# Dilated attention beside Strassen projections on one core: visits four steps later, the factors' transposition last in a visit, its read-back issued by POOL

## The chip, the cores and the metric

One Trainium2 chip; the kernel runs on one of its cores. The engines of a core that matter here are PE (TensorE, matrix products), DVE (VectorE) and ACT (ScalarE, both elementwise), POOL (GpSimd, which here mostly issues DMAs) and SP (SyncE, which only issues DMAs). The metric is the time of one execution in microseconds (us), the median of several runs.

## The reference

One layer of a bidirectional encoder over 1024 positions with 1024 features, in float32. Attention in three groups of four heads (window and dilation 128/1, 512/4, 2048/16) and a gated linear attention are mixed, followed by a squared-ReLU MLP. Cut to the part that matters here:

```
for gi, (win, dil) in enumerate(ATTN_PAIRS):
    o_g, lse_g = _dilated_group(aq[:, :, hs], ak[:, :, hs], av[:, :, hs], bias, dil, k_side)
    outs.append(o_g)
    lses.append(lse_g)
mix_w = jax.nn.softmax(jnp.stack(lses, axis=0), axis=0)
y_attn = jnp.sum(mix_w[..., None] * jnp.stack(outs, axis=0), axis=0)
...
merged = (jax.nn.sigmoid(gate_a) * (y_attn @ w_attn_branch[l])
          + jax.nn.sigmoid(gate_g) * (y_gla @ w_gla_branch[l]))
x = _layernorm(ALPHA * x + merged @ w_out[l], ln1_g[l], ln1_b[l])
```

The three groups' outputs for a head are added with weights that follow from their softmax denominators. These weights are the "factors" of this document.

## The kernel before

**The large products.** All large products are made of float32 split into two parts (a high part of fewer bits, and the rest), so each logical product of a 128x128 block with 512 columns is three matmuls (lines 102 to 104). The projections of the input are done in pairs of 128-row blocks by Strassen's scheme: seven products of four blocks each, so a *step* is 12 matmuls on PE, and a pair has seven steps. The list `steps` holds 10 steps that are left of two first pairs, and then seven for each of 14 pairs, 108 in all. A step has sides to be prepared three steps ahead (sums on DVE, then the split: cast on ACT, difference on DVE, line 152), and its product leaves PSUM by DVE (line 646) or ACT (lines 651, 671) into a tile `cr` or `cu`; finished blocks go to DRAM (`spill`, line 625, SP). The raw weights `praw` and `pwhi` come by SP (line 612).

**The attention tiles.** The pairs that project queries and keys come first, group 2, then 1, then 0, and the pairs of the gates last. Beside the pairs from there on run 24 attention tiles, `att(g, t)`: group 2's eight tiles of 128 queries, then group 1's, then group 0's. A tile has eight parts. `load` fetches queries `aq` and keys `ak` from `spill` (line 776, POOL). `scores` fetches the values `av` (lines 787 to 801, POOL), multiplies queries with keys into PSUM `sc` (line 809), adds the bias and finds the maximum on DVE (line 815, into `e` and `sm`), and takes the exponential on ACT (line 820). `turned` transposes `e` on PE (line 832, into `tr`) and copies it to `et`. `values` multiplies it with the values on PE (line 847) into the PSUM tile `avp`, columns 0 and 1 of three. For groups 1 and 2 the result is stored as it is (line 861). For group 0 it is weighted: `W` holds the factors of all three groups for this tile, spread over the partitions; DVE multiplies its first part with the result in PSUM (line 863), the second and third part with the stored results of the other groups, read back into `R` (line 871), adds them (line 872, `mixed`), and POOL stores the sum (line 873, `yadr`).

**The factors.** For a tile of group 0, `weigh` and `shares` work out the factors from the denominators in a chain of small DVE operations (lines 884 to 900, tile `f`). `spread` transposes them on PE (line 905) into column 2 of the same PSUM tile `avp`, ACT copies them to `fT` (line 906) and stores them in DRAM (line 907, `fdr`, issued by ACT); `loadw` reads them back into `W`, each row spread over 64 partitions (line 913). `W` has one buffer.

**The order.** A *visit* `visit(i)` does one part each of neighbouring tiles: `load` of tile i+1, `spread` of i-1, `values` of i-2, `scores` of i and `turned` of i-1. There are 26 visits; visit i stands ahead of the step whose number is given by a formula, from step 25 to step 96, every two or three steps. `weigh` comes one step after the visit, `shares` two, `loadw` of tile i-1 one, and from visit 17 on, every second visit, `quarter` (line 929, SP) reads the others' results for two tiles. The matmuls keep the written order by being told after which instruction they may issue (`issued["pe"]` is the last matmul of a large product, `issued["small"]` the last of a visit); other engines take their work in an order that the scheduler of the framework sets at build time, each engine in order. `W` was read back by SP.

**After the pairs.** One step after the last pair but one ends, the attention's memory is given up, and the tiles `ya` (from `yadr`) and `yg` for the merge are read and split beside the last seven steps (line 1002, SP). The merge then multiplies them with the branch weights.

Of the kernel before, what the change touches and what calls it, by code (L numbers as in the profile page):

```python
# [72 lines left out]
def build(tc, io):  # L73
    nc = tc.nc
    V, G, A, T, SP = nc.vector, nc.gpsimd, nc.scalar, nc.tensor, nc.sync
    P = Pools(tc)
    issued = {}
# [109 lines left out]
    for k in range(KT):  # L187
        n = {0: 1, 1: 1, 2: 2, 4: 2, 6: 2}.get(k)
# [532 lines left out]
    a, b = p0["steps"][1], p0["steps"][4]  # L721
# [30 lines left out]
    R, W = ap_.tile([128, 2, 2, 256], F32, name="R"), ap_.tile([128, 3, 2, 128], F32, name="W")  # L752
# [15 lines left out]
    def att(g, t):  # L768

        w, b0, k0 = window(g, t)  # L770
        b = {}
# [129 lines left out]

        def spread():
            if g == 0:
                with tc.issue_after(issued["pe"].ins):
                    issued["small"] = T.transpose(av[0:12, 2], b["f"][:, 0:3].rearrange("p g h -> p (g h)"), ident)
                A.copy(fT, av[0:12, 2])
                A.dma_start(fdr[t].rearrange("i r n -> r i n"), fT)

        def loadw():
            if g == 0:  # L910
                for i in range(2):
                    one = fdr[t, i:i + 1].rearrange("i r n -> i (r n)")
                    SP.dma_start(W[64 * i:64 * i + 64].rearrange("p g b n -> p (g b n)"), one.to_broadcast([64, 768]))

        return load, scores, turned, values, weigh, shares, spread, loadw

    def stats(g):
        for u in range(2):
            G.dma_start(s12[:, 4 * u:4 * u + 4, g - 1],
                        smdr[g - 1, 512 * u:512 * u + 512].rearrange("(t p) w -> p t w", p=128))  # L920

    def quarter(n):
        u, q = n // 2, n % 2
        for g in (1, 2):
            c = ORD[g]
            for pr in range(2):
                src = numdr[g - 1, pr].rearrange("p (c u q j) -> p u q c j", c=c, u=2, q=2)[:, u, q]
                dst = R[:, g - 1, pr].rearrange("p (c j) -> p c j", c=c)
                SP.dma_start(dst, src)
# [31 lines left out]

    def visit(i):

        for n, part in ((i + 1, 0), (i - 1, 6), (i - 2, 3), (i, 1), (i - 1, 2)):
            if 0 <= n < 24:
                tiles[n][part]()
        if i in (12, 16):
            stats(2 if i == 12 else 1)


    n0 = len(steps) + 14
    for p in projs[2:]:
        steps += p["steps"]
    n1 = len(steps) - 7
    units = {}
    for i in range(26):
        n = n0 + 1 + i * (n1 - n0) // 27
        units.setdefault(n, []).append(lambda i=i: visit(i))
        for k, part, later in ((i, 4, 1), (i, 5, 2), (i - 1, 7, 1)):
            if 0 <= k < 24 and (later == 1 or k > 15):  # L980
                units.setdefault(n + later, []).append(lambda k=k, part=part: tiles[k][part]())
        if i in (17, 19, 21, 23):
            units[n + 1].append(lambda i=i: quarter((i - 17) // 2))
    for i in range(8):

        n = n0 - 18 + i * 3 // 2
# [839 lines left out]
def make(arrays):  # L1826
    import concourse.bacc as _bacc
    nc = _bacc.Bacc("TRN2", target_bir_lowering=False, num_devices=1, dynamic_dma_scratch_size=1024)
    io = {}
    for n, a in arrays.items():  # L1830
        io[n] = nc.dram_tensor(f"in_{n}", a.shape, mybir.dt.from_np(a.dtype), kind="ExternalInput").ap()
    io["out"] = nc.dram_tensor("out_0", (S, D), F32, kind="ExternalOutput").ap()
    with tile.TileContext(nc, schedule_with_timeline_sim=True) as tc:
        build(tc, io)
    return nc
# [8 lines left out]
```

## Time and profile before

| | us |
|---|---|
| median of 3 runs (1393.45 to 1394.84) | 1394.82 |
| the profiled execution | 1393.93 |
| its span, first to last instruction | 1392.1 |
| PE busy | 1360.8 |
| DVE busy | 1008.3 |
| ACT busy | 629.5 |
| POOL busy | 105.1 |

The visits run from 299 us (the first scores) to 578 us (the last values) of the span. The page of the profile has the busy time of each engine, and the chain of work that ended last. The view of waits adds up, for each engine, who it waited for, and the timeline gives single instructions with their start, their duration and the idle time ahead of them with its releaser in square brackets. A row with "x8" stands for eight instructions in a row. An instruction that waits for several results is put down to the one that came last. The durations of matmuls overlap, since they are pipelined: the distance from one start to the next is what one costs. The mean granted clock of PE over the span is 0.993 of full speed.

### The profile page before, as it was taken

The numbers are of one execution on the slowest core, as the hardware profiler recorded it, in microseconds if no ns is written. First come the engines' busy times: TensorE is split into PE (matmuls) and PEld (weight loads), VectorE is DVE, ScalarE is ACT, GpSimd is POOL, SyncE is SP. The second block draws the span as 40 slices with busy tenths as digits, with TensorE's granted clock in tenths as the row PEclk, the third lists the DMA queues.
The fourth block names the chain that finished last, engine by engine and source line by source line (L and its number), as shares of the span: only waits on it lengthen the run. The fifth ranks groups of instructions, "written<-read, shape, count | busy, mean of one in ns | idle before, by whom it ended". The sixth has DMA issues, their size and how long they took to land.

```text
span 1392.1 us, 19096 instructions
## 1 busy us (share of the span) xinstructions
PE 1360.8 (98%) x6829; PEld 1133.4 (81%) x6829; DVE 1008.3 (72%) x1748; ACT 629.5 (45%) x1207; POOL 105.1 (8%) x157
## 2 busy tenths in 40 slices
PE   9999999979999998999999999999999999999998
PEld 7989998857877776788888888888888888888886
DVE  6377768756566576577666787788867897786988
ACT  5346645324444343354426655555556533333333
POOL 0000100022333221000001000000000000000002
PEclk9999999989999999999999999999999999999999
DMA  7262326755455564565763655666555965545313
GB/s 255 61 204 71 120 79 218 201 168 154 149 157 170 152 179 134 155 214 184 265 236 112 237 192 186 228 217 213 199 216 160 359 224 166 163 122 165 102 35 121
DMA packets 119747, 241.77 MB, mean 174 GB/s; under 512 B 33269, under 2 KB 42133, under 8 KB 119652
## 3 DMA queue, kind: packets, MB, share of 16 engines
q1 hardware_dynamic: 113044, 223.71, 48.8%
q0 software_dynamic: 6176, 16.39, 4.0%
q8 instruction: 54, 0.88, 0.3%
q10 hardware_dynamic: 432, 0.44, 0.1%
q14 instruction: 41, 0.34, 0.1%
HBM read 163.81 MB, written 77.73 MB: 174 GB/s over the span
## 4 chain that ended last, share of the span: by engine, by line
PE 93%; DVE 3%; ACT 2%; DMA 1%; issue 1%; SPq 0%; ACTq 0%; DVEq 0%; POOLq 0%
PE ps L102 18%; PE ps L103 18%; PE ps L104 18%; PE mm L102 10%; PE mm L103 10%; PE mm L104 10%; PE sc L809 2%; PE avp L847 2%; PE tr L832 2%; ACT xr L1235 1%; PE sc L409 0%; PE tr L379 0%; DVE cr L646 0%; DMA pwhi<-in_wfm 0%; DMA spill<-cr 0%
## 5 line engine op out<-in xcount | busy, mean ns | idle before, releaser
L1216 ACT CAST T<-hp 128x1024 fp32r<-128x1024 f32 x36 | 37.9, 1052 | 109.9 <-PE ps L103 70.4
L103 PE MATMUL mm<-wlo,x 128*128 128x272 f32 (+1 forms) x240 | 74.5, 311 | 0.7 <-DVE wlo L95 0.7
L102 PE MATMUL mm<-whi,x 128*128 128x272 f32 (+1 forms) x240 | 75.0, 313 | 0.0
L104 PE MATMUL mm<-whi,x 128*128 128x272 f32 (+1 forms) x240 | 74.7, 311 | 0.0
L820 ACT ACTIVATE e<-e,sm 128x256 f32<-128x256 f32 (+2 forms) x96 | 43.3, 453 | 68.2 <-DVE sm L815 59.5
L103 PE MATMUL ps<-B,B 128*128 128x512 f32 x160 | 62.2, 389 | 0.0
L104 PE MATMUL ps<-B,B 128*128 128x512 f32 x160 | 62.2, 389 | 0.0
L102 PE MATMUL ps<-B,B 128*128 128x512 f32 x160 | 60.9, 390 | 0.5 <-ACT B L1216 0.5
L103 PE MATMUL ps<-T,T 128*128 128x512 f32 x144 | 56.0, 389 | 0.0
L104 PE MATMUL ps<-T,T 128*128 128x512 f32 x144 | 56.0, 389 | 0.0
L102 PE MATMUL ps<-B,T 128*128 128x512 f32 x144 | 56.0, 389 | 0.0
L104 PE MATMUL ps<-B,T 128*128 128x512 f32 x144 | 56.0, 389 | 0.0
L103 PE MATMUL ps<-B,T 128*128 128x512 f32 x144 | 56.0, 389 | 0.0
L102 PE MATMUL ps<-T,T 128*128 128x512 f32 x144 | 56.0, 389 | 0.0
L1217 DVE TENSOR_TENSOR T<-hp,T 128x1024 fp32r<-128x1024 f32 x36 | 43.9, 1219 | 15.1 <-ACT T L1216 15.0
L1617 DVE TENSOR_TENSOR acc<-ps,acc 128x512 f32<-128x512 f32 x68 | 45.5, 683 | 12.8 <-PE ps L104 12.2
L646 DVE TENSOR_TENSOR cr<-cu,mm 128x512 f32<-128x512 f32 x44 | 35.2, 800 | 25.5 <-PE mm L104 25.3
L1722 POOL TENSOR_TENSOR mv<-mv,mhalf 128x1 f32<-128x1 f32 x8 | 7.0, 881 | 607.3 <-DVE mv L1721 605.8
L102 PE MATMUL mm<-x,pwlo 128*128 128x512 f32 x128 | 50.7, 396 | 1.4 <-ACT cu L651 1.4
L102 PE MATMUL ps<-T,fraw 128*128 128x512 f32 x128 | 49.6, 390 | 0.4 <-ACT T L1216 0.4
L103 PE MATMUL mm<-x,pwlo 128*128 128x512 f32 x128 | 49.9, 390 | 0.0
L104 PE MATMUL mm<-x,pwlo 128*128 128x512 f32 x128 | 49.9, 390 | 0.0
(498 smaller groups left out, 4191.1 us busy)
## 6 DMA issues: line engine op xcount, KB each, us to landing
hdr<-c SPq DMA_DIRECT2D x112, 256.0 KB, 2.2
hp<-hdr SPq DMA_DIRECT2D x56, 512.0 KB, 3.5
spill<-cr SPq DMA_DIRECT2D x64, 256.0 KB, 3.3
praw<-in_wfm SPq DMA_DIRECT2D x16, 512.0 KB, 5.4
pwhi<-in_wfm SPq DMA_DIRECT2D x16, 512.0 KB, 5.0
gate<-spill SPq DMA_DIRECT2D x32, 256.0 KB, 3.7
wa<-in_w SPq DMA_DIRECT2D x16, 512.0 KB, 5.3
wb<-in_w SPq DMA_DIRECT2D x16, 512.0 KB, 7.2
```

What stands on the lines that cost most here:

```text
L102: T.matmul(ps, lh, rh, start=first and i == 0, stop=False, skip_group_check=more)
L103: T.matmul(ps, lh, rl, start=False, stop=False, skip_group_check=more)
L104: issued["pe"] = T.matmul(ps, ll, rh, start=False, stop=last and i == n - 1, skip_group_check=more)
L646: issued["add"] = V.tensor_tensor(o, a, b, op=OP.add)
L809: mm = T.matmul(sps[i][:, pr, 0:w], q[ps_, pr], k[ps_, pr, 0:w], start=True, stop=True)
L820: issued["exp"] = A.activation(e, e, AF.Exp, bias=sm[:, h:h + 1], scale=-1.0, accum_out=sm[:, 4 + h:5 + h])
L832: T.transpose(tp[0:hi - lo, pr, j], b["e"][i][:, pr, lo:hi], ident)
L847: return T.matmul(av[64 * i:64 * i + 64, pr], vv[:, h * 64:h * 64 + 64], b["et"][i][p0:p0 + vv.shape[0], pr, j], start=j == pr == 0, stop= ...
L1216: A.copy(o[:, 0], src)
L1217: V.tensor_tensor(o[:, 1], src, o[:, 0].bitcast(F32), op=OP.subtract)
L1235: A.activation(q[i][:, k], tp[:, k], AF.Identity, bias=cols[:, c + 8:c + 9], scale=cols[:, c:c + 1])
L1617: V.tensor_tensor(m, p, m, op=OP.add)
```

## The change

Three edits. The formula of the visits' steps now begins at n0 + 5 in place of n0 + 1 and ends four steps later, at step 100; the two lines below are all of it. In a visit, `spread` of tile i-1 moves from second to last place, and its matmul is ordered after the visit's last small one instead of after the last large one. The read-back of the factors is issued by POOL instead of SP.

```
-                with tc.issue_after(issued["pe"].ins):
+                with tc.issue_after(issued["small"].ins):
                     issued["small"] = T.transpose(av[0:12, 2], b["f"][:, 0:3].rearrange("p g h -> p (g h)"), ident)
...
-                    SP.dma_start(W[64 * i:64 * i + 64].rearrange("p g b n -> p (g b n)"), one.to_broadcast([64, 768]))
+                    G.dma_start(W[64 * i:64 * i + 64].rearrange("p g b n -> p (g b n)"), one.to_broadcast([64, 768]))
...
-        for n, part in ((i + 1, 0), (i - 1, 6), (i - 2, 3), (i, 1), (i - 1, 2)):
+        for n, part in ((i + 1, 0), (i - 2, 3), (i, 1), (i - 1, 2), (i - 1, 6)):
...
-        n = n0 + 1 + i * (n1 - n0) // 27
+        n = n0 + 5 + i * (n1 - 6 - n0) // 25
```

What moves is seen in the built programs, whose rows stand in the order in which an engine takes them (line, operation, output and inputs, shape).

On PE, where the first scores stand (`x` and `xT` are the split input, `pw` and `px` the sides of a pair). Before:

```order
L104 MATMUL mm<-xT_2101,pwlo 128x512
...
L102 MATMUL mm<-x_94,px 128x512
...
L104 MATMUL mm<-x_94,px 128x512
L809 MATMUL sc<-ak_2251,aq_2248 128x128 x4
L102 MATMUL mm<-xT_2207,pwhi 128x512
```

And with the change:

```order
L104 MATMUL mm<-x_94,px 128x512
L102 MATMUL mm<-xT_2207,pwhi 128x512
...
L102 MATMUL mm<-xT_2086,pwhi 128x512
...
L104 MATMUL mm<-xT_1981,pwlo 128x512
L809 MATMUL sc<-ak_2251,aq_2248 128x128 x4
L102 MATMUL mm<-xT_2101,pwlo 128x512
```

The scores of the first tile stand behind 48 large matmuls more: the 1302 of the pairs that were ahead of them are 1350 now. All visits move by about as much; the last values stand behind 2202 in place of 2154.

On PE, in a visit of group 0 (the fourth with a transposition of factors). Before:

```order
L104 MATMUL mm<-xT_2224,pwhi 128x512
L905 MATMUL avp<-ident,f_2267 12x128
L847 MATMUL avp<-et_2260,av_2253 64x128
L847 MATMUL avp<-et_2261,av_2253 64x128
...
L809 MATMUL sc<-ak_2251,aq_2250 128x256 x4
L832 MATMUL tr<-ident,e_2258 128x128 x4
L832 MATMUL tr<-ident,e_2259 128x128 x4
L102 MATMUL mm<-x_93,pwlo 128x512
```

With the change:

```order
L104 MATMUL mm<-xT_1981,pwlo 128x512
L847 MATMUL avp<-et_2260,av_2253 64x128
L847 MATMUL avp<-et_2261,av_2253 64x128
...
L809 MATMUL sc<-ak_2251,aq_2250 128x256 x4
L832 MATMUL tr<-ident,e_2258 128x128 x4
L832 MATMUL tr<-ident,e_2259 128x128 x4
L905 MATMUL avp<-ident,f_2267 12x128
L102 MATMUL mm<-xT_2101,pwlo 128x512
```

The transposition now stands behind the visit's 8 matmuls of values, 4 of scores and 8 transpositions, and the large matmuls stand behind it. Between two transpositions stand 36 large matmuls, and once 24, before and now.

On ACT, in the same visit, around the copy of the factors and their store. Before:

```order
L651 COPY cu_2105<-mm 128x512
L906 COPY fT<-avp 12x128
L907 DMA fdr<-fT 6x2x128
L820 ACTIVATE e_2256,sm_2265<-e_2256,sm_2265 128x256 x2
L839 COPY et_2260<-tr 128x512
L820 ACTIVATE e_2257,sm_2265<-e_2257,sm_2265 128x256 x2
L888 ACTIVATE f_2266<-f_2266 128x12
```

With the change:

```order
L839 COPY et_2260<-tr 128x512
L820 ACTIVATE e_2256,sm_2265<-e_2256,sm_2265 128x256
L906 COPY fT<-avp 12x128
L820 ACTIVATE e_2256,sm_2265<-e_2256,sm_2265 128x256
L820 ACTIVATE e_2257,sm_2265<-e_2257,sm_2265 128x256 x2
L907 DMA fdr<-fT 6x2x128
L151 CAST pwlo<-pwhi 128x512
```

The copy and the store stood ahead of the four exponentials of the visit's scores; the store now stands behind all four. In the other visits it stands behind two to four of them, and in the last behind none, as there are no scores. On DVE L863 still stands ahead of the L815 of the same visit that those exponentials need.

## The prediction

> **What bounds the kernel now.** I read the page first, then the sum of waits of PE, then PE's timeline around each long wait.
>
> ```profile
> span 1392.1 us, 19096 instructions
> PE 1360.8 (98%) x6829; PEld 1133.4 (81%) x6829; DVE 1008.3 (72%) x1748; ACT 629.5 (45%) x1207; POOL 105.1 (8%) x157
> PE 93%; DVE 3%; ACT 2%; DMA 1%; issue 1%; SPq 0%; ACTq 0%; DVEq 0%; POOLq 0%
> ```
>
> PE is the bound from end to end: it is busy 98% of the span and carries 93% of the chain that ended last. A change that adds or removes no matmul can only move the 31 us in which PE is idle, and the time in which its clock is low. The next view lists the waits of PE, longest sum first (total, times, longest):
>
> ```profile
> PE sc L809 <- DMA ak<-spill: 9.6, 1, 9.6
> PE avp L905 <- DVE f L900: 7.2, 5, 2.2
> PE avp L847 <- ACT fT L906: 4.1, 8, 1.0
> PE mm L102 <- ACT cu L651: 1.4, 1, 1.4
> ```
>
> All four lie between 290 and 580 us. The first is the wait of the first scores for their keys; the next two are the transposition of the factors at the head of a visit, and the values that follow it. Each of the three belongs to an edit.
>
> **Edit 1: the visits begin four steps later.** In PE's timeline (start, duration, instruction, idle time before it):
>
> ```profile
> 289.41 0.39 PE L104 MATMUL mm<-x,px 128*128 128x512 f32 x1
> 299.40 1.23 PE L809 MATMUL sc<-ak,aq 64*128 64x128 f32 x8 [9.61 <-DMA ak<-spill]
> 300.56 0.79 PE L102 MATMUL mm<-xT,pwhi 128*128 128x512 f32 x1
> 304.43 0.39 PE L102 MATMUL mm<-xT,pwhi 128*128 128x512 f32 x1
> 307.96 0.71 PE L809 MATMUL sc<-ak,aq 64*128 64x128 f32 x8
> 308.61 0.66 PE L832 MATMUL tr<-ident,e 128*128 128x128 f32 x4
> 463.67 0.48 PE L102 MATMUL mm<-xT,pwlo 128*128 128x512 f32 x1
> 471.74 0.39 PE L104 MATMUL mm<-x,px 128*128 128x512 f32 x1
> 296.59 1.43 POOL L776 DMA_DIRECT2D ak<-spill  x2 [8.52 <-DMA spill<-cr]
> ```
>
> The 36 matmuls from 463.67 to 471.74 run undisturbed, so one costs 8.07 / 35 = 0.23 us and a step of twelve 2.75 us. Four steps are 48 matmuls, 11.0 us; as the rows of the order show, exactly these 48 now stand ahead of the first scores. PE would come to them at 289.8 + 11.0 = 300.8. The keys' load is issued by POOL at 296.59, when the projections have landed in DRAM; neither that projection nor its load is moved, and the scores began at 299.40. So the wait goes, with 1.4 us to spare. After it the clock was low: nine matmuls took 304.43 - 300.56 = 3.87 us where 2.07 is usual, and the scores 1.16 us to the next start where 0.65 is usual: 2.3 us. **Edit 1 is worth 9.6 + 2.3 = 11.9 us.** The matmuls put in between hide the load; should the write or the load be later by more than 1.4 us, the rest is waited for again.
>
> At the far end the last visit moves from 12 steps before the end of the projections to 8, which is 96 matmuls or 22 us of cover for what follows it: three products on DVE, the write of the mixed tile and its reading by the merge. Before, SP had these reads behind twelve steps; I cost this at nothing, as the two DMAs (under 5 us each, by the rows of DMAs below) and some 4 us of DVE need about 14. Without that cover the merge would wait for the difference.
>
> **Edit 2: the transposition last in a visit.** Here are the first, one middle and the last of the eight visits that have it:
>
> ```profile
> 473.75 0.28 PE L905 MATMUL avp<-ident,f 128*12 128x128 f32 x1 [1.62 <-DVE f L900]
> 474.37 1.49 PE L847 MATMUL avp<-et,av 128*64 128x128 f32 x16 [0.34 <-ACT fT L906]
> 475.79 2.08 PE L809 MATMUL sc<-ak,aq 64*128 64x256 f32 x8
> 512.64 0.27 PE L905 MATMUL avp<-ident,f 128*12 128x128 f32 x1
> 513.25 1.09 PE L847 MATMUL avp<-et,av 128*64 128x128 f32 x16 [0.34 <-ACT fT L906]
> 516.19 0.47 PE L102 MATMUL mm<-x,pwlo 128*128 128x512 f32 x1
> 566.22 0.28 PE L905 MATMUL avp<-ident,f 128*12 128x128 f32 x1 [0.86 <-DVE f L900]
> 577.10 1.24 PE L847 MATMUL avp<-et,av 128*64 128x128 f32 x16
> ```
>
> A visit without waits takes 516.19 - 512.64 - 0.34 = 3.2 us, so from one transposition to the next PE needs 8.3 + 3.2 = 11.5 us where 36 matmuls lie between, and 8.8 where 24 do, which happens once. Seven intervals should take 6 x 11.5 + 8.8 = 77.8 us; 473.75 to 566.22 is 92.5. With the 1.6 before the first, these visits lose 16.3 us: idle time, and low clock after some of it (scores of 2.08 us where 1.1 is usual). Last in the visit, the transposition comes 3 us later, past the longest wait for L900 (2.2), and the values find the copy of fT long done. Of the 16.3 only the 1.4 of L651 has no link to the edit, so **14.9 us go**.
>
> But a new wait takes their place. Values and factors share one PSUM tile: that is why L847 waits for the copy of fT above. So the transposition must now wait until DVE has read the values that stand just ahead of it (L863), and L863 needs W of that tile. W is what the transposition of the visit before wrote, copied, stored and read back. This ring has to close within one interval. On ACT the store (L907) moves behind the exponentials of the same visit, which wait for DVE's L815, which stand behind L863. The rows:
>
> ```profile
> 502.61 0.42 DVE L863 TENSOR_TENSOR W<-avp,W 128x256 f32<-128x256 f32 x1
> 504.88 0.51 ACT L820 ACTIVATE e<-e,sm 128x256 f32<-128x256 f32 x1 [3.52 <-DVE sm L815]
> 506.85 0.49 ACT L820 ACTIVATE e<-e,sm 128x256 f32<-128x256 f32 x1
> 474.35 1.30 ACTq L907 DMA_DIRECT2D fdr<-fT  x1
> 478.00 1.12 SPq L913 DMA_DIRECT2D W<-fdr  x2
> 566.82 0.71 ACTq L907 DMA_DIRECT2D fdr<-fT  x1
> 567.40 0.95 SPq L91 DMA_DIRECT2D raw<-in_wb  x2
> SPq L913 <- DMA fdr<-fT: 0.2, 1, 0.2
> 518.04 0.43 DVE L872 TENSOR_TENSOR mixed<-W 128x256 f32<-128x256 f32 x1
> 518.87 0.73 POOL L873 DMA_DIRECT2D yadr<-mixed  x1 [1.56 <-DVE sm L815]
> W<-fdr SPq DMA_DIRECT2D x16, 192.0 KB, 4.2
> av<-vdr POOLq DMA_DIRECT2D x5, 256.0 KB, 3.1
> ak<-spill POOLq DMA_DIRECT2D x4, 256.0 KB, 4.6
> ```
>
> From L863 to the end of the fourth exponential is 507.3 - 502.6 = 4.7 us; in half of the visits L907 stands behind fewer of them or one DVE operation less, so 4.5. The store takes between 1.7 us (568.35 + 0.2 - 566.82, where SP came late to its wait) and 3.65 (474.35 to 478.00); I take the middle, 2.7. POOL picks up a result 518.87 - 518.47 = 0.4 us after it is there. The first of two W loads is issued for 0.73 us, and the second lands after 3.1 to 4.6 us by other loads of POOL, 4.2 by SP's own; no row shows W from POOL, so I take 3.6. **The ring is 4.5 + 2.7 + 0.4 + 0.7 + 3.6 = 11.9 us**, between 10.4 and 13.9. Against the intervals: the first is covered (its L907 hangs on no L863, 0.7 us spare), the short one waits 11.9 - 8.8 - 0.7 = 2.4, five others 0.4 each: 4.4, and 1.7 of low clock after the long one (as the visit at 473.75 lost some 1.6 after 1.62 idle). **The ring costs 6.1 us**; at 10.4 about nothing, at 13.9 some 18 and low clock on top.
>
> DVE too stands still while L863 waits, with everything behind it:
>
> ```profile
> 500.00:520.00 20.00, 18.52 (x119) 14.75 (x120) 16.10 (x55) 7.62 (x25) 5.80 (x8) 1.00 0.70 201
> ```
>
> 16.1 us of work in 20 (the third number after the window's length) leaves some 2 us per interval, about what the ring takes; behind L863 are sums and splits for matmuls of at least one step later, so I add nothing.
>
> **Edit 3: POOL issues the read-back.** SP loses 16 issues and its waits for them; nothing on PE waited for SP, so the gain is nothing. On POOL the loads stand behind the store of the mixed tile of the same visit (4 us after L863 at most, while the store of fT lands at 7.2) and ahead of loads that are needed a visit later. POOL is busy 5.8 of 20 us.
>
> [...]
>
> **Sum.** 11.9 + 14.9 - 6.1 = 20.7 us. The profiled execution took 1393.93 us, 1.8 more than its span; the median of the runs is 1394.82, so 0.9 above it. 1394.8 - 20.7 gives **1374 us**.
>
> **Rivals.**
> 1. The ring hides (10.4 us): only the low figure of the store speaks for it. 11.9 + 14.9, less a rest of 1: 1369.
> 2. The ring is long (13 us): the store lands late beside SP's large loads, as at 474.35, W as late as ak. Waits: 0.4 + 4.2 + 5 x 1.5 = 12.1, low clock 4 or 5: 17 in place of 6, 1385.
> 3. Edit 1 does not do what it says: SP's queue or the loads put in front make the keys late by as much again, and the first scores wait at their new place. Against it: that projection, its store and POOL's load keep their order. Gain 14.9 - 6.1 = 9: 1386.
> 4. Slower: POOL, in order, comes to W only when an earlier DMA has landed. The nearest row:
>
> ```profile
> 509.88 0.73 POOL L873 DMA_DIRECT2D yadr<-mixed  x1 [4.41 <-DVE f L898]
> 505.10 0.42 DVE L872 TENSOR_TENSOR mixed<-W 128x256 f32<-128x256 f32 x1
> ```
>
> There POOL was 4.4 us late for a result of 505.5. Once per visit this makes the ring 16.3: waits of 3.7 + 7.5 + 5 x 4.8 = 35 and some 9 of low clock, 44 against the 26.8 removed: 1412. It decides from a ring of 14 to 15 us on. Of eight such stores one was that late, so it is unlikely for all.
>
> **Chances.** Forecast (1371 to 1381) 0.52, ring hidden 0.20, long ring 0.13, first wait stays 0.08, slower 0.07. 0.2% is 2.8 us, about what a measurement of this kernel can tell from no change. Faster by more than that: the first four but 0.02 of the long ring, 0.91; within it 0.03; slower 0.06. The range goes from 1367, where all the idle time of these visits is gone (28 us), to 1388; above lie the slower case and the worst of the long ring.
>
> **What would show it.** Step 1: no wait of L809 for ak, and full clock from 290 to 310. Step 2: no wait of L905 for L900 nor of L847 for L906, but one of L905 for L863, longest at the visit after 24 matmuls, and DVE idle ahead of L863 until W has landed. The distance from one L863 to the next, some 12 us, is the ring; from 14 on I am wrong in size, from 15 in sign. Step 3: POOL's W loads start 0.4 us after the store of fT has landed. A wait of the first product of the merge for ya would show the far end uncovered.

## The result, and the profile after

| | before | after |
|---|---|---|
| median, us | 1394.13 (4 runs, 1393.43 to 1394.84) | 1376.13 (4 runs, 1374.96 to 1376.83) |
| the profiled execution, us | 1393.93 | 1376.83 |
| its span, us | 1392.1 | 1375.0 |

The ratio is 0.9870, with a 95% interval of 0.9853 to 0.9887: 18 us less, against a forecast of 20.7 and a time of 1374. The head of the page after:

```profile
span 1375.0 us, 19093 instructions
PE 1359.5 (99%) x6829; PEld 1132.6 (82%) x6829; DVE 1008.8 (73%) x1748; ACT 630.0 (46%) x1207; POOL 113.7 (8%) x173
```

PE's busy time is what it was, and the span is nearer to it by 16 us: the time came from PE's idle time and its low clock, as foretold. The waits of PE after, longest sum first (total, times, longest):

```profile
PE avp L905 <- DVE W L863: 4.9, 2, 2.5
PE mm L102 <- DVE cu L646: 1.4, 1, 1.4
```

The wait for the keys (9.6), that for L900 (7.2) and that for L906 (4.1) are gone. What stands there is the wait of L905 for L863, twice. The stages show where the time went. These windows of before give length, busy PE, PEld, DVE, ACT and POOL, then PE's granted clock, the share of the DMA engines and GB/s:

```profile
234.00:290.00 56.00, 55.79 (x246) 45.68 (x244) 44.79 (x69) 19.00 (x34) 4.00 (x6) 1.00 0.72 218
290.00:465.00 175.00, 165.60 (x954) 132.00 (x955) 101.13 (x277) 71.05 (x213) 58.60 (x86) 0.97 0.48 146
465.00:580.00 115.00, 102.36 (x588) 79.93 (x586) 79.04 (x258) 40.48 (x117) 17.81 (x25) 0.97 0.54 158
```

And the same windows after:

```profile
234.00:290.00 56.00, 54.62 (x241) 44.75 (x240) 43.29 (x67) 18.58 (x33) 3.47 (x5) 1.00 0.70 208
290.00:465.00 175.00, 174.72 (x1001) 139.32 (x1000) 107.80 (x279) 73.05 (x213) 57.60 (x85) 1.00 0.51 160
465.00:580.00 115.00, 110.10 (x631) 87.67 (x630) 83.71 (x275) 46.14 (x129) 28.70 (x45) 0.97 0.56 162
```

In the stage from 290 on, where groups 2 and 1 are visited, PE's idle time falls from 9.4 us to 0.3 and the clock rises from 0.97 to 1.00. In the stage with group 0, idle time falls from 12.6 to 4.9 us, but the clock stays at 0.97. The window ahead of both, which lies ahead of the visits, has 1.2 us more of idle time after. PE's timeline after, at the first scores, at the first large matmul behind visit 16 (the last visit ahead of group 0's factors), at six of the eight transpositions of group 0's visits, and at the first large matmul behind visit 25, the last:

```profile
303.18 0.71 PE L809 MATMUL sc<-ak,aq 64*128 64x128 f32 x8
465.59 0.48 PE L102 MATMUL mm<-xT,pwhi 128*128 128x512 f32 x1
488.53 0.27 PE L905 MATMUL avp<-ident,f 128*12 128x128 f32 x1
499.88 0.27 PE L905 MATMUL avp<-ident,f 128*12 128x128 f32 x1 [2.47 <-DVE W L863]
512.90 0.27 PE L905 MATMUL avp<-ident,f 128*12 128x128 f32 x1
526.93 0.28 PE L905 MATMUL avp<-ident,f 128*12 128x128 f32 x1 [2.43 <-DVE W L863]
539.99 0.27 PE L905 MATMUL avp<-ident,f 128*12 128x128 f32 x1
551.21 0.27 PE L905 MATMUL avp<-ident,f 128*12 128x128 f32 x1
571.15 0.50 PE L102 MATMUL mm<-x,px 128*128 128x512 f32 x1
```

The end of the same stretch before:

```profile
578.28 0.50 PE L102 MATMUL mm<-x,pwlo 128*128 128x512 f32 x1
```

From 539.99 to 551.21 nothing waits: 11.22 us is what 36 large matmuls and a visit take. After each of the two waits the next distance is longer than that by 1.8 us (13.02, 13.06): low clock, granted at 0.53 from 500.46 to 504.10 and from 527.74 to 531.39. The first wait stands at the interval with 24 large matmuls. Each "distance" here is from the start of one transposition to the start of the next.

The distance from the first transposition to the last is no fair measure, because the transposition has changed its place in the visit and so other work lies in between. The *stretch of group 0's visits* is: from the first large matmul behind visit 16 to the first behind visit 25 the work of PE is the same in both kernels. It took 114.6 us before (463.67, a row shown in the prediction, to 578.28) and takes 105.6 us after (465.59 to 571.15).

What the parts gave in these two executions: PE was 2.6 us late by 285 already, as the same product started at 284.06 before and at 286.66 after. With that, and the 48 matmuls of the edit (10.9 us), the first scores would have come at 312.9; they came at 303.18, so 9.7 us is gained there, and 1.9 from there to the second scores (8.56 us before, 6.70 after). **The first two visits gave 11.6 us**; edit 1 was foretold at 11.9. **The visits of group 0 gave 9.0 us**; edit 2 was foretold at 8.8. Together 20.6; less the 2.6 lost ahead of them and 0.9 behind them, this is the 17.1 us between the spans. These are the gains of two stages, and not yet those of two edits: the next section shows that edit 1 also shortens the second stage.

### The profile page after: what moved, and what is told of

It is laid out like the page before. It is cut to its first block, busy times and chain, and to the rows that moved or that the text cites. A ratio compares the mean times of both kernels' runs of the same rounds, so it can differ in the third digit from the quotient of the medians.

```text
span 1375.0 us, 19093 instructions
## 1 busy us (share of the span) xinstructions
PE 1359.5 (99%) x6829; PEld 1132.6 (82%) x6829; DVE 1008.8 (73%) x1748; ACT 630.0 (46%) x1207; POOL 113.7 (8%) x173
## 4 chain that ended last, share of the span: by engine, by line
PE 61%; ACT 1%; DMA 1%; issue 1%; DVE 1%; POOL 0%; POOLq 0%; DVEq 0%; ACTq 0%
PE ps L102 18%; PE ps L103 18%; PE ps L104 18%; PE mm L102 2%; PE mm L104 2%; PE mm L103 2%; ACT xr L1235 1%; DMA pwhi<-in_wfm 1%; PE ps L1232 0%; PE avp L847 0%; PE ps L1743 0%; DMA W<-fdr 0%; DMA fdr<-fT 0%; PE tr L832 0%; PE ps L1739 0%
## 5 line engine op out<-in xcount | busy, mean ns | idle before, releaser
L102 PE MATMUL mm<-whi,x 128*128 128x272 f32 (+1 forms) x240 | 75.0, 312 | 0.0
L102 PE MATMUL ps<-B,B 128*128 128x512 f32 x160 | 61.0, 390 | 0.5 <-ACT B L1216 0.5
L646 DVE TENSOR_TENSOR cr<-cu,mm 128x512 f32<-128x512 f32 x44 | 35.3, 802 | 32.4 <-PE mm L104 32.2
L102 PE MATMUL ps<-T,T 128*128 128x512 f32 x144 | 56.1, 389 | 0.0
L102 PE MATMUL ps<-B,T 128*128 128x512 f32 x144 | 56.1, 389 | 0.0
L102 PE MATMUL mm<-x,pwlo 128*128 128x512 f32 x128 | 51.5, 402 | 1.4 <-DVE cu L646 1.4
L102 PE MATMUL ps<-T,fraw 128*128 128x512 f32 x128 | 49.6, 390 | 0.4 <-ACT T L1216 0.4
```

The costliest lines, as they stand in the source:

```text
L102: T.matmul(ps, lh, rh, start=first and i == 0, stop=False, skip_group_check=more)
L646: issued["add"] = V.tensor_tensor(o, a, b, op=OP.add)
```

## The experiments

### Which edit gives what

Each of four kernels has some of the three edits and nothing else.

Edit 1 alone: the kernel before with

```
-        n = n0 + 1 + i * (n1 - n0) // 27
+        n = n0 + 5 + i * (n1 - 6 - n0) // 25
```

> Only the visits begin four steps later; the transposition of the factors stays first, SP reads them back. By the two traces the first scores lose their wait of 9.6 us and 1.9 us of low clock, 11.6 us in all, and the eight visits of group 0 keep what they lost before: 1394.1 - 11.6 = 1382.5 us, within 1.5. Rival: the late start also brings the last visits nearer to the merge or upsets SP's queue, and part is given back: 1385 or more. Rival: edit 1 carries nearly all of the gain: 1377 or less.

Edits 2 and 3: the changed kernel with the line above undone.

> The transposition last in a visit and the read-back by POOL, with the visits at their old steps. The first scores wait for their keys as before (9 to 10 us). In the eight visits of group 0 the traces show 17.4 us of waits and low clock gone and 8.4 come (two waits of L905 for L863, 2.5 us each, and 1.8 of low clock behind each): 1394.1 - 9.0 = 1385.1 us, within 1.5. Rival: the two edits help only with the late start: 1390 or more.

Edits 1 and 2: the changed kernel with

```
-                    G.dma_start(W[64 * i:64 * i + 64]...
+                    SP.dma_start(W[64 * i:64 * i + 64]...
```

> The changed kernel with the read-back issued by SP again. The prediction has edit 3 at nothing: 1376 us, within 1. Rival: SP, in order, waits for the store of fT, which now lands later than before, with raw weights and stores queued behind it, or comes to it late from them; W lands 2 us or more later, the ring closes in 13 to 14 us, L905 waits for L863 in most visits: 1382 to 1386.

Edits 1 and 3: the changed kernel with `spread` second in a visit again, ordered after `issued["pe"]`.

> The changed kernel with the transposition of the factors first in a visit again. The 17.4 us of the group-0 visits come back (waits of L905 for L900, of L847 for L906) and the 8.4 of the ring go: 1376.1 + 9.0 = 1385.1 if POOL's read-back helps nothing; by the run with edit 1 alone the same 1382.5 to 1385. Rival: the waits for L900 came of SP's W loads and POOL's load removes part of them: 1380 or less.

| edits | median, us | runs from to | ratio to before | 95% interval | stretch of group 0's visits, us |
|---|---|---|---|---|---|
| none | 1394.55 | 1393.07 to 1395.29 | 1 | | 114.6 |
| 1 | 1381.41 | 1378.82 to 1382.74 | 0.9906 | 0.9891 to 0.9922 | 109.5 |
| 2, 3 | 1387.04 | 1385.69 to 1390.19 | 0.9950 | 0.9938 to 0.9963 | 106.6 |
| 1, 2 | 1381.31 | 1376.81 to 1383.00 | 0.9899 | 0.9883 to 0.9916 | 108.7 |
| 1, 3 | 1387.87 | 1386.21 to 1388.21 | 0.9951 | 0.9939 to 0.9964 | 118.5 |
| 1, 2, 3 | 1376.13 | 1374.96 to 1376.83 | 0.9870 | 0.9853 to 0.9887 | 105.6 |

The time without edits was taken beside the four partial kernels; all three edits were measured earlier, against 1394.13. The last column is read from the one profiled execution of each kernel, over the stretch defined above.

Edit 1 alone gives 13.1 us, by its interval 10.9 to 15.2. Edits 2 and 3 without it give 7.5 (5.2 to 8.6), a little under what was expected. These would add up to 20.6, and all three give 18.0, because they overlap: edit 1 alone was expected to leave the visits of group 0 as they were, but takes 5.1 us off their stretch. Edits 2 and 3 take 8.1 us off it without edit 1, and 3.9 on top of edit 1. Why the later steps help these visits was not followed up.

On top of edit 1, edit 3 alone costs 6.5 us (9.0 in the stretch), and edits 2 and 3 together give 5.3 (3.9 in the stretch). Edit 2 alone gives nothing by the medians (0.8 in the stretch). This last is the least sure: the five runs with edits 1 and 2 lie 6 us apart, the fastest of them (1376.81, the profiled one) is about as fast as the changed kernel, and the two intervals overlap a little. That edit 3 is worth nothing is wrong: without edit 2 it costs, and with edit 2 it gains by the medians, and by 3.1 us in the stretch.

Why edit 3 alone costs time is seen in PE's rows around one transposition. With edit 1 alone:

```profile
511.52 0.27 PE L905 MATMUL avp<-ident,f 128*12 128x128 f32 x1
523.55 0.27 PE L905 MATMUL avp<-ident,f 128*12 128x128 f32 x1
536.05 0.27 PE L905 MATMUL avp<-ident,f 128*12 128x128 f32 x1
```

With edits 1 and 3:

```profile
511.88 0.27 PE L905 MATMUL avp<-ident,f 128*12 128x128 f32 x1
529.30 0.38 PE L905 MATMUL avp<-ident,f 128*12 128x128 f32 x1 [5.23 <-DVE f L900]
542.96 0.27 PE L905 MATMUL avp<-ident,f 128*12 128x128 f32 x1
```

These two intervals are 6.6 us longer, of the 9.0 by which all eight visits are longer in these two executions. On DVE, in the kernel with edits 1 and 3, the sum of the raw weights L633 stands there ahead of the last two operations of the factors, L899 and L900 (the last is shown):

```profile
527.75 0.69 DVE L633 TENSOR_TENSOR psum<-pwhi 128x512 f32<-128x512 f32 x1 [4.65 <-DMA pwhi<-in_wfm]
529.08 0.17 DVE L900 TENSOR_TENSOR f<-f 128x12 f32<-128x12 f32 x1
```

And with edit 1 alone it stands behind them:

```profile
522.99 0.17 DVE L900 TENSOR_TENSOR f<-f 128x12 f32<-128x12 f32 x1
526.71 0.69 DVE L633 TENSOR_TENSOR psum<-pwhi 128x512 f32<-128x512 f32 x1 [3.56 <-DMA pwhi<-in_wfm]
```

The raw weights are late in both (3.6 and 4.7 us of waiting). In one the factors are done ahead of this wait, in the other they stand behind it. The read-back itself stands in neither chain: its engine made the scheduler write DVE's list in another order, and these few rows are the only difference between DVE's lists in the two programs (L639, an operation on the same raw weights, moves with L633).

### Edit 3: the order on DVE, or POOL's issue

With edits 1 and 2, L863 stood at one place ahead of L898 to L900 of the next tile, and L905 waited 4.9 us for L900. The next kernel is that one, with L863 told to issue behind the last L900:

```
+                issued["fac"] = V.tensor_tensor(f[:, 0:3], f[:, 0:3], f[:, 4:5]...
...
-            o = V.tensor_tensor(W[:, 0], av[:, 0:2], W[:, 0], op=OP.mult)
+            with tc.issue_after(issued.get("fac", issued["add"]).ins): o = V.tensor_tensor(W[:, 0], av[:, 0:2], W[:, 0], op=OP.mult)
```

> The kernel with edits 1 and 2 (SP issues the read-back), and one thing more: L863 is told to issue behind the last L900. Only one place of DVE's list changes by it: there L863, which waits for W, stood ahead of L898 to L900 of the next tile, and L905 waited 4.9 us for L900. Now these stand ahead of it, as with POOL's read-back. Theory: edit 3 gained by the order on DVE alone: 1376 us as with all three edits, at least 3 us below the 1381.3 of the kernel with edits 1 and 2. Rival: POOL's own issue, off SP's queue, is what gains: 1381 stays.

Measured: 1377.12 us (1374.87 to 1380.20), ratio 0.9879, 0.9865 to 0.9892. The median falls by 4.2 of the 5.2 us, but the intervals of the two kernels overlap, and their profiled executions took 1376.62 and 1376.81 us. The trace does not bear the theory out. PE's row at that place, with edits 1 and 2:

```profile
500.43 0.38 PE L905 MATMUL avp<-ident,f 128*12 128x128 f32 x1 [4.92 <-DVE f L900]
```

And with the forced order:

```profile
498.75 0.38 PE L905 MATMUL avp<-ident,f 128*12 128x128 f32 x1 [3.88 <-DVE W L863]
```

The wait for L900 is gone, and one for W, 1.0 us shorter, has its place: SP's two issues of W took 1.84 us there, and L863 waited 4.5 us for W to land (the slowest load of W in that kernel took 5.3 us, the median 3.4). With POOL the wait of L905 was 2.47. So at this place, in these executions, 1.0 us goes with the order and 1.4 with the read-back itself; the rest of the 5 us is within the spread of these runs (6 us with edits 1 and 2). Over the stretch of group 0's visits the forced order takes 108.3 us, against 108.7 without it and 105.6 with POOL: 0.4 of 3.1 us. What edit 3 gains on top of edits 1 and 2 is therefore not shown to be the order on DVE; how it divides stays open.

### The ring of W: its length

The ring is the chain from one L863 through the exponentials, the store of the factors and their read-back into `W` to the next L863.

All engines' timeline of the kernel after, along the ring into the first wait:

```profile
487.28 0.42 DVE L863 TENSOR_TENSOR W<-avp,W 128x256 f32<-128x256 f32 x1 [0.30 <-DMA W<-fdr]
490.89 0.42 DVE L815 CUSTOM_DVE_ANT_0 e<-sc,strip 128x256 f32<-128x256 f32 x1
491.86 0.24 ACT L906 COPY fT<-avp 12x128 f32<-12x128 f32 x1
492.73 0.73 ACTq L907 DMA_DIRECT2D fdr<-fT  x1
493.80 0.42 DVE L872 TENSOR_TENSOR mixed<-W 128x256 f32<-128x256 f32 x1
494.71 0.73 POOL L873 DMA_DIRECT2D yadr<-mixed  x1 [5.13 <-DMA fdr<-fT]
495.44 1.07 POOL L913 DMA_DIRECT2D W<-fdr  x2
499.40 0.42 DVE L863 TENSOR_TENSOR W<-avp,W 128x256 f32<-128x256 f32 x1 [2.48 <-DMA W<-fdr]
```

From L863 to L863 it is 12.1 us, as foretold (11.9): 5.45 to the store, 2.7 to POOL's issue, 0.5, and 3.4 until W is there. But a second path ends at the same place. POOL comes to W only behind the store of `mixed`, whose L872 reads the W that is to be overwritten: this store is issued 7.4 us after L863, where the prediction had 4 at most, and W 8.2 us after L863. Besides, the copy L906 itself stands behind an exponential, which stands behind L815. So the next kernel, which takes L907 from behind the exponentials, tells whether the store is what counts:

```
-                A.dma_start(fdr[t].rearrange("i r n -> r i n"), fT)
+                G.dma_start(fdr[t].rearrange("i r n -> r i n"), fT)
```

> The changed kernel with the store of fT issued by POOL in place of ACT, where it stood behind the exponentials: the ring loses the 2 to 5 us from L906 to L907; DVE's list stays the same at these places. Theory: the short interval is then covered but for at most 0.5 us, and the second wait of L905 goes as its echo: 1368 to 1370 us. Rival: the ring is ruled by the loads' landing (3.1 to 6.6 us) and by POOL's order, the waits stay: 1375 to 1378. Rival: the second wait stays alone: 1372.

Measured: 1378.05 us (1376.01 to 1378.42), ratio 0.9881, 0.9867 to 0.9894. The waits of L905 for L863 are still there (3.1 us at this place), and the time is at the upper end of the rival's range: the rival is right. Its rows at the same place:

```profile
490.20 0.42 DVE L863 TENSOR_TENSOR W<-avp,W 128x256 f32<-128x256 f32 x1 [2.47 <-DMA W<-fdr]
493.64 0.24 ACT L906 COPY fT<-avp 12x128 f32<-12x128 f32 x1
494.28 0.59 POOL L907 DMA_DIRECT2D fdr<-fT  x1 [3.97 <-ACT fT L906]
497.14 1.07 POOL L913 DMA_DIRECT2D W<-fdr  x2
502.16 0.42 DVE L863 TENSOR_TENSOR W<-avp,W 128x256 f32<-128x256 f32 x1 [3.50 <-DMA W<-fdr]
```

L906 is held up here as there; the store comes 0.4 us after it in place of 0.6, POOL comes to W 2.9 us after that, behind the store of `mixed`, and the ring is 12.0 us, as long as before. What a copy of fT ahead of the exponentials together with a second buffer of W would bring was not tried.

### The first wait: the short interval

Three kernels move visits by steps and leave all else. The first was meant to take the short interval out of group 0:

```
+        n = n0 + 5 + i * (n1 - 6 - n0) // 25 - (12 <= i < 22)
```

> The changed kernel with visits 12 to 21 one step earlier, so that the interval with 24 large matmuls lies between visits 11 and 12, ahead of group 0, and all intervals of group 0 have 36. Theory: the ring of W closes in 11 to 12 us, so only the short interval waits for W (L905 2.5 us and 1.8 of low clock behind it), and the second wait of L905 is an echo of it: DVE came late by it, freed the raw weights late and then waited for the next ones. Both go: 1376.1 - 8.4 = 1368 us, within 2. Rival: the second wait comes of the raw weights alone and stays: 1372. Rival: the ring is longer than 36 matmuls allow in other visits too, or a wait for the factors (L900) comes instead, since DVE's list now has two operations on raw weights ahead of one L900: 1376 or more.

What the expectation says of the intervals does not hold. The short interval of group 0 lies between visits 18 and 19 and is not touched by moving both; what changes is that visits 12 to 21 come one step earlier, and the interval from 21 to 22 gets 48 matmuls. Measured: 1373.29 us (1370.61 to 1375.41), ratio 0.9849, 0.9835 to 0.9863. The first wait stayed (2.56 us), the second was gone. The next kernel does what the first was meant to, with `(12 <= i < 19)`:

> The changed kernel with visits 12 to 18 one step earlier and nothing else: now the interval between visits 18 and 19 has 36 large matmuls like all others of group 0, and visits 19 to 25 stand where they stood. Measured ring of W at this place in the changed kernel: 12.1 us from one L863 to the next. Theory: the first wait of L905 for L863 goes (2.5 us and 1.8 of low clock), and the second goes as its echo, since DVE is no longer late when it reaches the raw weights: 1376.1 - 8.4 = 1368 us, within 2. Rival: the second wait comes of the raw weights' place at that step alone and stays: 1372. Rival: the ring is longer than 36 matmuls allow, and nothing goes: 1375 or more.

Measured: 1373.14 us (1371.81 to 1373.72), ratio 0.9850, 0.9833 to 0.9866. Its transpositions:

```profile
495.22 0.27 PE L905 MATMUL avp<-ident,f 128*12 128x128 f32 x1 [0.38 <-DVE W L863]
521.62 0.37 PE L905 MATMUL avp<-ident,f 128*12 128x128 f32 x1 [3.08 <-DVE W L863]
```

The first wait falls from 2.47 to 0.38: it is the short interval against a ring of 12 us. The second does not go with it. It is no echo, which was the theory behind both of these runs.

### The second wait: one place in DVE's list, and a slow load

DVE at the second wait in the kernel after:

```profile
525.84 0.69 DVE L633 TENSOR_TENSOR psum<-pwhi 128x512 f32<-128x512 f32 x1 [3.31 <-DMA pwhi<-in_wfm]
526.45 0.42 DVE L863 TENSOR_TENSOR W<-avp,W 128x256 f32<-128x256 f32 x1
```

L863 stands behind L633, which waits for raw weights. Both moves of visits together, `- (5 <= i < 22) - (12 <= i < 19)`:

> As the run before, with visits 5 to 21 one more step earlier, so that the interval from visit 21 to 22 has 48 large matmuls and L863 of visit 21 stands ahead of the sum of the late raw weights on DVE, as in the run with visits 12 to 21 moved, where the second wait was gone. Theory: no wait of L905 is left: 1367 to 1369 us; if the second wait was an echo the same as the run before, if not, 4 us below it. Rival: with the visits a step earlier the raw weights stand ahead of another L863, and a wait moves there: 1371 to 1374.

Measured: 1370.84 us (1368.04 to 1372.24), ratio 0.9830, 0.9813 to 0.9846. The rival's mechanism is right, though the time lies just below its 1371 to 1374: the second wait has gone from its place, and one of 3.39 us has come at 497.39, where in this kernel another L633 with late raw weights (DVE waits 4.27 us) stands ahead of L863. So the last kernel leaves the visits as in the one with `(12 <= i < 19)` and changes only this one place of DVE's list; the other engines' lists stay as they are:

```
-                    V.tensor_tensor(st["s"], w[1, 0], w[1, 1], op=OP.add)
+                    with tc.issue_after(issued["ws"][3].ins) if len(issued.get("ws", ())) == 7 else nullcontext(): V.tensor_tensor(st["s"], w[1, 0], w[1, 1], op=OP.add)
...
-            o = V.tensor_tensor(W[:, 0], av[:, 0:2], W[:, 0], op=OP.mult)
+            o = V.tensor_tensor(W[:, 0], av[:, 0:2], W[:, 0], op=OP.mult); issued.setdefault("ws", []).append(o)
```

> The kernel with even intervals (visits 12 to 18 one step earlier) and one thing more: at one place of DVE's list the sum of the late raw weights (L633) is told to issue behind L863 and L871 of the visit, ahead of which it stood; no other engine's list changes. In the run before, DVE stood 3.7 us before this L633 and L905 waited 3.1 us for the L863 behind it, with some 1.7 of low clock after it. Theory: the second wait is this place in DVE's list and nothing else, and goes: 1373.1 - 4.8 = 1368.3 us, within 1.5, no L905 waiting for L863 by more than 0.5. Rival: the sum comes 2 us later and the large products wait for it in place of L905, a new wait of L102 or L103 for a split side: 1372 to 1374. Rival: W lands late there too, and the wait stays in part: 1371.

Measured: 1371.16 us (1369.64 to 1371.73), ratio 0.9827, 0.9814 to 0.9841: 2.0 us of the 4.8, with intervals that overlap slightly. The third case is right. PE and DVE there:

```profile
521.91 0.42 DVE L863 TENSOR_TENSOR W<-avp,W 128x256 f32<-128x256 f32 x1 [3.23 <-DMA W<-fdr]
522.39 0.28 PE L905 MATMUL avp<-ident,f 128*12 128x128 f32 x1 [2.01 <-DVE W L863]
535.19 0.28 PE L905 MATMUL avp<-ident,f 128*12 128x128 f32 x1 [1.20 <-DVE W L863]
```

With L633 out of the way L863 waits for W itself. The landing of this one load (shortest, median, longest of its two issues, us) in the kernel after, and the window around it:

```profile
DMA to landing us min/median/max: 5.6/6.1/6.6
517.00:525.00 8.00, 7.50 (x52) 5.70 (x50) 4.50 (x15) 2.42 (x6) 2.76 (x5) 1.00 0.86 227
```

All 16 issues of W in the kernel after:

```profile
DMA to landing us min/median/max: 3.1/3.3/6.6
```

It takes 6.1 us where 3.3 is the median. In the same 8 us SP fetches 1 MB of raw weights, and the DMA engines are busy 86% of the time (56% over the stage). So the second wait has two causes, one hidden behind the other: with L633 out of the way, the landing of W still holds up 2.0 of the 3.1 us. The other half, W on time and L633 left in its place, was not tried, and that it is the raw weights that make W late is argued from the time at which they come and from no run. In the kernel with the last edit the ring takes 13.6 us there (the L863 ahead of this one stands at 508.32).

### The spare of edit 1

All visits one step earlier, `n0 + 4`:

> The changed kernel with all visits one step (12 large matmuls, 2.7 us) earlier. Theory: the keys' load lands when it did, at most 1.4 us ahead of PE by the prediction, so the first scores wait for it 1.3 to 2.7 us, with some 1.5 of low clock behind: about 1379 to 1380 us if the rest stays. Rival: the load has more cover than that, no wait of L809 for ak: 1376. What the shift by a step does to the waits of group 0 beside this is not foretold; the wait of L809 is read from the profile by itself.

Measured: 1377.86 us (1375.76 to 1379.41), ratio 0.9881, 0.9867 to 0.9896. The first scores wait:

```profile
301.06 0.71 PE L809 MATMUL sc<-ak,aq 64*128 64x128 f32 x8 [3.02 <-DMA ak<-spill]
```

With 2.7 us less in front, the wait is 3.0: the spare of four steps is about nothing, not 1.4. Seven of the ten other kernels that begin at `n0 + 5` show it too, with waits for `ak` of 0.4 to 1.2 us.

### An order that tests nothing

The visit's parts in the order scores, `spread`, `turned`, `values`, so that L905 would wait for no L863:

> The changed kernel with the order scores, transposition of the factors, transposition of e, values in a visit: the transposition comes 1.1 us after the visit's start, and stands ahead of the values, so it waits for no L863 of its own visit; the copy of fT is hidden behind the transposition of e. Theory: the waits of L905 for L863 go (8.4 us with their low clock), the waits for L900 of the kernel before come back less 1.1 us each (some 2 us): 1376.1 - 8.4 + 2 = 1370 us, within 2. Rival: the factors come later on DVE than before, since POOL's read-back changed its list, and L905 waits for L900 as in the run with edits 1 and 3: 1378 to 1385.

Measured: 1422.37 us (1420.69 to 1425.73), ratio 1.0207, 1.0193 to 1.0221. The expectation overlooked that `et` has three buffers and a tile takes two: with `turned` ahead of `values`, the transposition of the next tile is copied over a half that the values still need, so this kernel works the values out from another tile's `et`. Most of its extra time is a new wait for that copy, 34 us in three rows, of which this is the largest:

```profile
PE avp L847 <- ACT et L839: 23.5, 14, 6.8
```

It says nothing about the ring.

## Why the prediction was right, and where it was not

- **What bounds the kernel: right.** All of the gain is PE's idle time and low clock; its busy time did not move (1360.8 and 1359.5 us).
- **Edit 1, 11.9 us: right for the first scores, but not all that it does.** 11.6 in the trace at the first two visits. "Each of the three belongs to an edit" does not hold: in the kernel with edit 1 alone the stretch of group 0's visits is 5.1 us shorter as well, a part of what the prediction had put down to edit 2. **"1.4 us to spare" was wrong:** the spare is about zero. The keys' load was issued 3.7 us later after (300.32 to 296.59), of which 2.6 is PE's own lateness there. The far end did cost nothing: no product of the merge waits for ya.
- **Edit 2, the waits that go: right.** No wait of L905 for L900 nor of L847 for L906 is left. 14.9 us was foretold to go, and with the gain of 9.0 and two waits of 2.45 with 1.8 behind each, 17.5 must have gone, part of it by edit 1: an undisturbed interval takes 11.2 us, not the 11.5 by which the loss was worked out, and the 1.4 us of L651 that the prediction kept is not there after either.
- **Edit 2, the new ring: right in its length, short by one place.** Foretold 11.9 us; measured 12.1 into the first wait, in part by luck: the store came 1.0 us later after L863 than foretold, and all behind it took 0.7 less. This wait was 2.5 us where 2.4 was foretold, at the interval with 24 matmuls and with 1.8 of low clock (foretold 1.7). The five small waits of 0.4 did not come, and a second long one did, with its own low clock: 4.2 us. The cost was 8.5 in place of 6.1. Two steps failed there. W was priced at 3.6 us from issue to landing for all tiles: true of seven of the eight, and 6.1 for the one that is loaded beside the raw weights. And the sentence that adds nothing for DVE's own lateness looked at what stands behind L863, not at L633, which stands ahead of it. A third, that the store of the mixed tile comes 4 us after L863 at most, was wrong at the first wait, where it is 7.4; it did no harm, as the other path is as long.
- **Edit 3, nothing: wrong in mechanism, without harm to the sum.** The edits were priced apart, as if the order of each engine's list were given. On top of edit 1, edit 3 without edit 2 costs 6.5 us, most of it by one exchange on DVE, and edit 2 without edit 3 gives nothing by the medians, for a reason that stays open. The prediction compared the lists of before and after, but not what each edit alone does to them. That nothing on PE waited for SP's issue was true of the kernel before; with edits 1 and 2 W comes from SP and is itself in the ring.
- **POOL's issues and loads of W, with DVE busy 73% of the stage:** the 16 issues took 522 to 547 ns, and 14 of them landed in 3.1 to 4.0 us. The late load does not point to DVE: it was busy 4.5 of the 8 us around it, less than that share, and of the loads that SP issued in the kernel with the forced order the slowest took 5.3 us.
- **The sum.** 20.7 foretold, 20.6 in these two stages; 18.0 by the medians, inside the forecast range. That the second stage came out (9.0 for 8.8) is luck: what went was 2.6 us more than foretold, and what the waits cost 2.4 more. In the profiled executions most of the rest lies outside the stages: PE was already 2.6 us late at 285, 1.4 of it in the wait of L102 for L646 in the list above, which stands at 262. The lists of instructions up to there are the same as in the kernel with `(12 <= i < 19)`, where PE was busy 56.00 of these 56 us (54.62 after) and has no such wait, so this is a spread of the executions and not of the change.

The best two of the kernels that were run, both with evened intervals, took 1370.84 and 1371.16 us, 5 us below the changed kernel.

## What to carry to other kernels

Where a scheduler orders each engine's list, an edit is priced by the lists it makes, not by its own work: an operation that waits for a DMA and stands one place ahead of a link of the critical chain can cost the whole wait (5.2 us here). Gains of edits that touch the same waits do not add up (13.1 and 7.5 us apart, 18.0 together). A ring over several engines is compared with the shortest interval between two turns, not with the mean, and each of its loads with what else is on the DMA engines at that moment (one load of W took 6.1 us where 3.3 was the median, with the DMA engines busy 86% of the time). When a wait shrinks by less than its cause was thought to be worth, look for a second cause that had been hidden behind it.

## What was not expected of the hardware

Low clock after a wait of PE came in a step in these kernels, not in proportion. With a distance of 11.22 us as the undisturbed one, nine waits of 2.3 to 3.4 us of L905 that stand alone, in eight kernels, were each followed by 1.8 us of loss, whatever their length, and four of 1.2 to 2.0 us by 0 to 0.4. In the kernel with the last edit, with four waits of 0.2 to 2.0 us, the granted clock of the stage was 1.00; in the one after, with two of 2.5, it was 0.97. A wait of 3.88 cost 2.7, and one of 4.92, in the kernel with edits 1 and 2, 2.6. The matmuls behind the first wait in the kernel after, the first and the last at low clock:

```profile
500.79 0.63 PE L102 MATMUL mm<-x,pwlo 128*128 128x512 f32 x1
...
503.35 0.63 PE L102 MATMUL mm<-x,pwlo 128*128 128x512 f32 x1
```

From 500.79 to 503.35 six steps take 0.43 us each in place of 0.23. The granted clock is 0.50 from 500.79 to 503.77, and 0.53 from 500.46 to 504.10, with the slower rows on either side: 47% of these 3.64 us are 1.7 us lost, near the 1.8 measured. It is no rule for all waits: in the kernel before, 1.62 us with another 0.34 close behind was followed by low clock (0.50 from 475.79 to 477.90). What sets the step was not tried.
